# Seven half-size products in part of the first matmul of a fused matmul, GELU, matmul kernel

## The chip, the cores and the metric

The kernel runs on one core of a Trainium2 chip. Times are device microseconds (us) of whole executions. A profiled execution also has a span, from its first to its last recorded instruction, which is some 1.8 us shorter than the time. In these kernels TensorE (PE) does matmuls, VectorE (DVE) and ScalarE (ACT) work elementwise, GpSimd (POOL) mainly issues DMAs, SyncE (SP) issues the rest. A matmul has a stationary operand, which a weight load (PEld in the profile; 577 of them beside 577 matmuls before the change) brings in, and a moving one; its result goes to a bank of PSUM (the `ps` tiles), from where VectorE or ScalarE fetches it. float32r is the 32-bit type that this kernel gives to the operands of products that read sums.

## The reference

```
h = a @ b                    # a 1024x1024, b 1024x2048, float32
h = gelu_tanh(h)
out = h @ c                  # c 2048x1024
```

The tanh form of GELU makes everything between the two products elementwise.

## The kernel before

The intermediate is kept transposed: the first product has b as the stationary operand and the transposed a as the moving one, so its results are tiles of the transposed h, which the second product takes without a transpose. `aT[0]` and `aT[1]` hold the two halves of a's rows, transposed, in bf16. The head loads a's first half and 768 columns of b in float32, casts and transposes, and runs six tiles of the first product k by k as b arrives:

```python
    N0 = 6
    W0 = N0 * 128
    ...
    b0stage = ctx.enter_context(tc.tile_pool(name="b0stage", bufs=8))
    ...
    for k in range(KT):
        if k + 1 < KT:
            cast_b0(k + 1)                      # VectorE casts one half, ScalarE the other
        for t in range(N0):
            nc.tensor.matmul(ps[t], bt(k, t), aT[0][:, k, :],
                             start=(k == 0), stop=(k == KT - 1))
```

The other columns of b, a's second half and c come by casting DMAs on GpSimd's queue. All 256 matmuls of the first product are plain bf16:

```python
    def mm1(t, h):
        p = ppool.tile([128, H], F32, name="ps")
        for k in range(KT):
            nc.tensor.matmul(p, bt(k, t), aT[h][:, k, :],
                             start=(k == 0), stop=(k == KT - 1))
        gelu(t, h, p)
    ...
    for t in range(N0 + N1, NT):                # t = 10 .. 15
        mm1(t, 0)
        if t == NT - 3:
            turn(0)                             # eight transposes on PE, one VectorE copy
        if t == NT - 2:
            turn(1)
            turn(2)
            turn(3)
```

The second product already uses the Winograd form of Strassen's scheme: both operands cut into 2x2 blocks, sums of blocks (`s1` to `s4`, `t1` to `t4`) formed first, and seven block products instead of eight. The sums are float32r tiles; five of the seven products read them, two read bf16 blocks. Its last part is ordered so that one row of output blocks is left, in three narrow pieces, for the end.

Of the kernel before, what the change touches and what calls it, by code (L numbers as in the profile page):

```python
# [9 lines left out]
F32 = mybir.dt.float32  # L10
# [9 lines left out]
def kernel(ctx, tc, a, b, c, out):  # L20
# [9 lines left out]
    W0 = N0 * 128  # L30
    N1 = 4
    W1 = N1 * 128

# [9 lines left out]
    b0stage = ctx.enter_context(tc.tile_pool(name="b0stage", bufs=8))  # L43
# [9 lines left out]
    NH = NT // 2  # L53
    aT = [keep.tile([128, KT, H], BF16, name=f"aT{h}", tag=f"A{h}") for h in range(2)]
    WB = W0 + W1
    b_lo = keep.tile([128, KT, WB], BF16, name="b_lo", tag="B0")
    b_hi = keep.tile([128, KT, N - WB], BF16, name="b_hi", tag="B1")

    def bcols(k0, kn, n0, w):
        if n0 < WB:  # L60
            return b_lo[:, k0:k0 + kn, ds(n0, w)]
        return b_hi[:, k0:k0 + kn, ds(n0 - WB, w)]

    def bt(k, t):
        return bcols(k, 1, t * 128, 128)[:, 0, :]


    hq = [[keep.tile([128, NH, H], F32R if h else BF16, name=f"h{h}{g}") for g in range(2)]
          for h in range(2)]
# [19 lines left out]
    for mt in range(4):  # L89
        load_a0(mt, 2 if mt == 3 else 1)  # L90
# [38 lines left out]
    for mt in range(4):  # L129
        if mt < 3:  # L130
            ab.append(cast_a0(mt + 1))
        turn0(mt, ab[mt], (0,) if mt == 3 else (0, 1))
        if mt < 3:
            warm_up(3)
    cast_b0(0)
    for k in range(KT):
        if k + 1 < KT:
            cast_b0(k + 1)
        for t in range(N0):
            nc.tensor.matmul(ps[t], bt(k, t), aT[0][:, k, :],  # L140
                             start=(k == 0), stop=(k == KT - 1))
# [3 lines left out]
    def gelu(t, h, p):  # L145
        nc.scalar.activation(hq[h][t // NH][:, t % NH, :], p, AF.Gelu_apprx_tanh)  # L146

    for t in range(N0):
        gelu(t, 0, ps[t])


    def load_b(k0, kn, n0, w):
        nc.gpsimd.dma_start(out=bcols(k0, kn, n0, w), in_=bv[:, k0:k0 + kn, ds(n0, w)])

    ps = [(tpool if t < 2 else ppool).tile([128, H], F32, name="pt" if t < 2 else "ps")
          for t in range(N1)]
    for k in range(0, KT, 4):
        load_b(k, 4, W0, W1)
        for i in range(4):
            for t in range(N1):  # L160
                nc.tensor.matmul(ps[t], bt(k + i, N0 + t), aT[0][:, k + i, :],  # L161
                                 start=(k + i == 0), stop=(k + i == KT - 1))
    for t in range(N1):
        gelu(N0 + t, 0, ps[t])


    def mm1(t, h):
        p = ppool.tile([128, H], F32, name="ps")
        for k in range(KT):
            nc.tensor.matmul(p, bt(k, t), aT[h][:, k, :],  # L170
                             start=(k == 0), stop=(k == KT - 1))
        gelu(t, h, p)

    W2 = 384
    for n0 in range(W0 + W1, N, W2):
        for k in range(0, KT, 4):
            load_b(k, 4, n0, W2)

    a1 = []
    for j in range(4):  # L180
        st = abf.tile([128, K], BF16, name="ab1")
        nc.gpsimd.dma_start(out=st, in_=av[:, 4 + j, :])
        a1.append(st)

    def turn(j):
        ab = a1[j]
        pt = tpool.tile([128, KT, 128], BF16, name="pt")
        for k in range(KT):
            nc.tensor.transpose(pt[:, k, :], ab[:, ts(k, 128)], ident)  # L189
        nc.vector.tensor_copy(aT[1][:, :, ts(j, 128)], pt)  # L190

    for t in range(N0 + N1, NT):
        mm1(t, 0)
        if t == NT - 3:
            turn(0)
        if t == NT - 2:
            turn(1)
            turn(2)
            turn(3)
# [7 lines left out]
    (h11, h12), (h21, h22) = hq  # L207
    c11 = keep.tile([128, NH, H], BF16, name="c11")
    c21 = keep.tile([128, NH, H], BF16, name="c21")
    c22 = keep.tile([128, NH, H], F32R, name="c22")  # L210
    c12 = keep.tile([128, NH, H], BF16, name="c12", tag="A0")
# [5 lines left out]
    load_c(c11, 0, 0)  # L217
    load_c(c22, 1, 1)
    load_c(c21, 1, 0)
    load_c(c12, 0, 1)  # L220
# [152 lines left out]
```

## Time and profile before

| | before |
|---|---|
| median time, first three runs | 123.97 us |
| span of the profiled execution | 122.1 us |
| PE busy | 95% of the span |
| first stage (six tiles, k by k) ends | 21.85 us |
| first product ends, second begins | 69.02 us |
| last matmul ends | 119.2 us |

The prediction below shows the page and the chain. The list of waits, cut to PE's own, stands behind the prediction: engine, line, what it waited for, total, times, longest.

```profile
PE ps L101 <- DVE warm L49: 1.2, 1, 1.2
PE ps L140 <- DVE b_lo L125: 0.8, 1, 0.8
PE pt L115 <- DVE aT L118: 0.7, 1, 0.7
PE pt L189 <- DVE aT L190: 0.3, 1, 0.3
```

The first three lie in the head, before 12 us. After it PE really idles once, for 0.3 us, before the transposes of line 189.

The table by half microseconds of the head: the last column is what the DMA engines moved, in GB/s.

```profile
4.50:5.00 0.50, 0.50 (x5) 0.49 (x5) 0.00 (x0) 0.12 (x1) 0.00 (x0) 1.00 0.96 303
...
6.50:7.00 0.50, 0.50 (x10) 0.40 (x8) 0.00 (x0) 0.00 (x0) 0.00 (x0) 1.00 0.83 279
...
9.50:10.00 0.50, 0.41 (x5) 0.21 (x3) 0.05 (x1) 0.50 (x2) 0.00 (x0) 1.00 0.89 237
...
12.50:13.00 0.50, 0.50 (x5) 0.21 (x3) 0.05 (x1) 0.50 (x2) 0.00 (x0) 1.00 1.05 424
```

From 4.5 to 10.5 us the loads run at 237 to 388 GB/s, 312 on average; from 11 to 15.5 us they hold 399 to 424.

### The profile page before, as it was taken

How to read it: one execution, taken by the hardware profiler on the slowest of the kernel's cores; microseconds unless marked ns; L12 is line 12 of the kernel's file. 1: busy time of each engine (PE TensorE's matmuls, PEld its weight loads, DVE VectorE, ACT ScalarE, POOL GpSimd, SP SyncE). 2: the span in 40 equal slices, each digit the busy share in tenths (PEclk: the TensorE clock that was granted, in tenths of full speed). 3: DMA queues.
4: the chain of work that ended last, by engine and by line, in shares of the span. 5: the costliest groups of instructions: out<-in, count | busy, mean ns of one | idle time of the engine just before them, and what ended most of it. 6: DMA issues, size and time to landing. Idle time of an engine off the chain costs nothing.

```text
span 122.1 us, 1486 instructions
## 1 busy us (share of the span) xinstructions
PE 116.1 (95%) x577; PEld 68.3 (56%) x577; DVE 64.6 (53%) x95; ACT 30.7 (25%) x54; POOL 21.5 (18%) x26
## 2 busy tenths in 40 slices
PE   6977999999998999999999999999999999999990
PEld 2542444444456444444444444468888888888880
DVE  0352340000014200006999999999769999974351
ACT  4454752806331133233323331100000000000000
POOL 2000099132440220000000000797000000000000
PEclk9999999999999999999999999999999999999999
DMA  3999969999999999995000000000600022445425
GB/s 144 351 328 347 413 188 191 198 200 205 209 207 206 329 394 231 206 206 97 0 0 0 5 0 3 3 0 0 258 0 0 5 86 86 157 167 191 163 99 167
DMA packets 12582, 18.44 MB, mean 151 GB/s; under 512 B 800, under 2 KB 7584, under 8 KB 12576
## 3 DMA queue, kind: packets, MB, share of 16 engines
q0 software_dynamic: 7968, 8.91, 39.6%
q1 hardware_dynamic: 4464, 9.37, 20.9%
q10 hardware_dynamic: 144, 0.07, 0.2%
q8 instruction: 4, 0.07, 0.2%
q14 instruction: 2, 0.02, 0.0%
HBM read 20.97 MB, written 4.19 MB: 206 GB/s over the span
## 4 chain that ended last, share of the span: by engine, by line
PE 88%; DMA 6%; SPq 2%; DVE 1%; ACT 0%; issue 0%
PE ps L273 41%; PE ps L170 31%; PE ps L140 8%; DMA b_st<-in_b_dram 6%; PE ps L161 3%; PE pt L161 3%; SPq L78 2%; PE pt L189 1%; DVE aT L190 1%; ACT b_lo L126 0%; SPq L85 0%; DVE ot L342 0%; PE pt L115 0%
## 5 line engine op out<-in xcount | busy, mean ns | idle before, releaser
L146 ACT ACTIVATE h<-ps 128x512 fp32r<-128x512 f32 (+1 forms) x30 | 17.3, 602 | 28.6 <-PE ps L170 26.3
L170 PE MATMUL ps<-aT,b_hi 128*128 128x512 bf16 x96 | 21.4, 379 | 0.0
L170 PE MATMUL ps<-aT,b_lo 128*128 128x512 bf16 x80 | 17.4, 379 | 0.0
L170 PEld LDWEIGHTS <-b_hi 128*128 128x128 bf16 x96 | 9.3, 98 | 10.8
L273 PE MATMUL ps<-t,s 128*128 128x512 f32 x64 | 15.0, 392 | 0.0
L273 PE MATMUL ps<-t,h 128*128 128x512 f32 x64 | 14.8, 389 | 0.0
L273 PE MATMUL ps<-c,h 128*128 128x512 bf16 (+2 forms) x80 | 14.2, 336 | 0.0
L313 POOL COPY lk<-u 128x512 f32<-128x512 f32 x1 | 7.7, 7684 | 33.6 <-ACT u L306 33.6
L273 PEld LDWEIGHTS ps<-t,s 128*128 128x128 f32 x64 | 12.0, 188 | 2.6
L273 PEld LDWEIGHTS ps<-t,h 128*128 128x128 f32 x64 | 12.0, 188 | 2.5
L170 PEld LDWEIGHTS <-b_lo 128*128 128x128 bf16 x80 | 7.8, 98 | 9.4
L227 DVE TENSOR_TENSOR t<-c,c 128x1024 fp32r<-128x1024 bf16 x4 | 4.7, 1222 | 15.8 <-DMA c<-in_c_dram 15.7
L190 DVE COPY aT<-pt 128x1024 bf16<-128x1024 bf16 x4 | 2.7, 689 | 19.4 <-PE pt L189 19.3
L140 PE MATMUL ps<-aT,b_lo 128*128 128x512 bf16 x48 | 10.9, 380 | 0.8 <-DVE b_lo L125 0.8
L273 PEld LDWEIGHTS <-h 128*128 128x128 bf16 x80 | 7.2, 98 | 7.0 <-issue 0.3
L140 PEld LDWEIGHTS <-b_lo 128*128 128x128 bf16 x48 | 4.5, 98 | 6.6 <-DVE b_lo L125 1.1
L215 POOL DMA_DIRECT2D c<-in_c_dram x8 | 5.9, 744 | 11.7 <-PE ps L170 6.0
L296 DVE TENSOR_TENSOR ot<-ps,u 128x512 f32<-128x512 f32 x11 | 7.3, 684 | 1.1 <-PE ps L273 1.1
L101 PE MATMUL ps<-warm 128*128 128x512 bf16 x17 | 6.3, 516 | 1.2 <-DVE warm L49 1.2
L273 PE MATMUL ps<-c,s 128*128 128x512 f32 x32 | 7.4, 389 | 0.0
L273 PEld LDWEIGHTS ps<-c,s 128*128 128x128 f32 x32 | 6.0, 188 | 1.2
L125 DVE CAST b_lo<-b_st 128x384 bf16<-128x384 f32 x8 | 2.9, 368 | 5.1 <-DMA b_st<-in_b_dram 5.1
(40 smaller groups left out, 96.5 us busy)
## 6 DMA issues: line engine op xcount, KB each, us to landing
out_dram<-ot SPq DMA_DIRECT2D x15, 256.0 KB, 2.0
c<-in_c_dram POOLq DMA_DIRECT2D x6, 512.0 KB, 14.8
b_st<-in_b_dram SPq DMA_DIRECT2D x7, 384.0 KB, 8.1
c<-in_c_dram POOLq DMA_DIRECT2D x2, 1024.0 KB, 15.0
a_st<-in_a_dram SPq DMA_DIRECT2D x3, 512.0 KB, 4.1
b_hi<-in_b_dram POOLq DMA_DIRECT2D x4, 384.0 KB, 11.3
b_lo<-in_b_dram POOLq DMA_DIRECT2D x2, 512.0 KB, 7.2
ab<-in_a_dram POOLq DMA_DIRECT2D x4, 256.0 KB, 13.9
```

What stands on the lines that cost most here:

```text
L101: nc.tensor.matmul(ps[N0 - 1], warm[:, 0:128], warm, start=True, stop=True)
L125: nc.vector.tensor_copy(b_lo[:, k, 0:HW], b_st[k][:, 0:HW])
L140: nc.tensor.matmul(ps[t], bt(k, t), aT[0][:, k, :], start=(k == 0), stop=(k == KT - 1))
L146: nc.scalar.activation(hq[h][t // NH][:, t % NH, :], p, AF.Gelu_apprx_tanh)
L161: nc.tensor.matmul(ps[t], bt(k + i, N0 + t), aT[0][:, k + i, :], start=(k + i == 0), stop=(k + i == KT - 1))
L170: nc.tensor.matmul(p, bt(k, t), aT[h][:, k, :], start=(k == 0), stop=(k == KT - 1))
L190: nc.vector.tensor_copy(aT[1][:, :, ts(j, 128)], pt)
L215: nc.gpsimd.dma_start(out=dst[:, t:t + 4, :], in_=cv[:, r * NH + t:r * NH + t + 4, ts(q, H)])
L227: nc.vector.tensor_tensor(t1[i], c12[:, ts(i, 2), :], c11[:, ts(i, 2), :], op=SUB)
L273: nc.tensor.matmul(p, lhs(t)[:, ts(j, 128)], rhs(t)[:, q], start=(t == 0), stop=(t == NH - 1))
L296: nc.vector.tensor_tensor(ot, u if swap else p, p if swap else u, op=op)
L313: nc.gpsimd.tensor_copy(last_keep, last)
```

## The change

The intent is fewer matmuls. The left half of the first product (1024 columns of b) stays plain, and all of it is now loaded in the head. The right half (1024 columns) is done as seven block products of 512x512x512, 16 matmuls each, 112 in place of 128. With A and B cut into blocks, `as1` = A21+A22, `as2` = A11-as1, `as3` = A11-A21, `b12` becomes T1 = B12-B11, `bt2` = T1-B22, `bt3` = B22-B12. Two sums get their second addend later, by a DMA that accumulates: `as2` += A12 and `bt2` += B21. The products are combined with VectorE adds from PSUM. In the second product the seven products stay, in another order; the sums t2 and t3 move from VectorE to ScalarE (a negated copy) plus an accumulating DMA, and t4 becomes a further accumulating DMA into t2.

The diff, cut to its core:

```diff
-    W0 = N0 * 128
+    W0 = N // 2                                # columns of b loaded in the head
-    b0stage = ctx.enter_context(tc.tile_pool(name="b0stage", bufs=8))
+    b0stage = ctx.enter_context(tc.tile_pool(name="b0stage", bufs=6))
     ...                                        # (cut: tiles)
+    for j in R:                                # a's second half, first on GpSimd's queue
+        nc.gpsimd.dma_start(out=st, in_=av[:, 4 + j, :])
+    nc.gpsimd.dma_start(out=b12, in_=bv[:, 0:KH, W0 + H:N])
+    nc.gpsimd.dma_start(out=b22, in_=bv[:, KH:KT, W0 + H:N])
     ...                                        # (cut: bx)
+    mm1(6, 0, h11[:, 6, :])
+    turn(0)
+    mm1(7, 0, h11[:, 7, :])
+    turn(1)
+    turn(2)
+    mm1_half(0, 0)                             # 256 columns: needs turn(0), turn(1) only
+    turn(3)
+    mm1_half(1, 0)
+    mm1_half(2, 0)
+    for t in range(3):
+        mm1_half(t, 1)
     ...                                        # (cut: twelve sums on VectorE, mm1 for t = 3 .. 7)
+    for j in R:                                # third product
+        p = bank()
+        prod(p, KH, pairs(bt2), pairs(as2), j)
+        tt(v2[:, j, :], p, v2[:, j, :], op=ADD)
+    for i in range(2):
+        nc.gpsimd.dma_start(out=as2[i], in_=aT[0][:, P2[i + 2], :], accum_op=ADD)
+    for i in range(2):
+        nc.gpsimd.dma_start(out=bt2[i], in_=bx[:, P2[i + 2], :], accum_op=ADD)
+    for j in R:                                # fourth
+        p = bank()
+        prod(p, KH, pairs(bt3), pairs(as3), j)
+        tt(v3[j], p, v2[:, j, :], op=ADD)
     ...                                        # (cut: sums for the second product)
+    for j in R:                                # fifth
+        p = bank()
+        prod(p, KH, whole(b12), pairs(as1), j)
+        add_gelu(h22[:, 4 + j, :], p, v3[j])
+        tt(v2[:, j, :], p, v2[:, j, :], op=ADD)
     ...
+    for j in R:                                # sixth: reads as2 again, with its second addend
+        p = bank()
+        prod(p, KH, whole(b22), pairs(as2), j)
+        add_gelu(h12[:, 4 + j, :], p, v2[:, j, :])
     ...                                        # (cut: seventh, bt2 x a22; the second product)
```

More of the change, by code (lines that the diff above doesn't have):

```diff
@@ L29 @@
     N0 = 6
-    W0 = N0 * 128
-    N1 = 4
-    W1 = N1 * 128
+    W0 = N // 2
+    KH = KT // 2
+    NH = NT // 2
+    R = range(4)
     av = a.rearrange("(mt p) k -> p mt k", p=128)
@@ L51 @@
     make_identity(nc, ident)
-    NH = NT // 2
     aT = [keep.tile([128, KT, H], BF16, name=f"aT{h}", tag=f"A{h}") for h in range(2)]
-    WB = W0 + W1
-    b_lo = keep.tile([128, KT, WB], BF16, name="b_lo", tag="B0")
-    b_hi = keep.tile([128, KT, N - WB], BF16, name="b_hi", tag="B1")
-    def bcols(k0, kn, n0, w):
-        if n0 < WB:
-            return b_lo[:, k0:k0 + kn, ds(n0, w)]
-        return b_hi[:, k0:k0 + kn, ds(n0 - WB, w)]
-    def bt(k, t):
-        return bcols(k, 1, t * 128, 128)[:, 0, :]
-    hq = [[keep.tile([128, NH, H], F32R if h else BF16, name=f"h{h}{g}") for g in range(2)]
-          for h in range(2)]
+    a22 = keep.tile([128, KH, H], F32R, name="a22", tag="A22")
+    b_lo = keep.tile([128, KT, W0], BF16, name="b_lo", tag="B0")
+    bx = keep.tile([128, KT, H], BF16, name="bx", tag="BX")
+    b12 = keep.tile([128, KH, H], F32R, name="b12", tag="BT")
+    b22 = keep.tile([128, KH, H], F32R, name="b22", tag="BR")
+    (h11, h12), (h21, h22) = [[keep.tile([128, NH, H], F32R if h else BF16, name=f"h{h}{g}")
+                               for g in range(2)] for h in range(2)]
     a_st, b_st = {}, {}
@@ L88 @@
     gate = consts.tile([128, 1], F32, name="gate")
-    for mt in range(4):
+    for mt in R:
         load_a0(mt, 2 if mt == 3 else 1)
@@ L128 @@
     ab = [cast_a0(0)]
-    for mt in range(4):
+    for mt in R:
         if mt < 3:
@@ L139 @@
         for t in range(N0):
-            nc.tensor.matmul(ps[t], bt(k, t), aT[0][:, k, :],
+            nc.tensor.matmul(ps[t], b_lo[:, k, ts(t, 128)], aT[0][:, k, :],
                              start=(k == 0), stop=(k == KT - 1))
@@ L143, with gelu, bank @@
             turn0(3, ab[3], (1,))
-    def gelu(t, h, p):
-        nc.scalar.activation(hq[h][t // NH][:, t % NH, :], p, AF.Gelu_apprx_tanh)
+    def gelu(dst, src):
+        nc.scalar.activation(dst, src, AF.Gelu_apprx_tanh)
+    def bank(w=H):
+        return ppool.tile([128, w], F32, name="ps", padded_shape=[128, H])
     for t in range(N0):
-        gelu(t, 0, ps[t])
-    def load_b(k0, kn, n0, w):
-        nc.gpsimd.dma_start(out=bcols(k0, kn, n0, w), in_=bv[:, k0:k0 + kn, ds(n0, w)])
-    ps = [(tpool if t < 2 else ppool).tile([128, H], F32, name="pt" if t < 2 else "ps")
-          for t in range(N1)]
-    for k in range(0, KT, 4):
-        load_b(k, 4, W0, W1)
-        for i in range(4):
-            for t in range(N1):
-                nc.tensor.matmul(ps[t], bt(k + i, N0 + t), aT[0][:, k + i, :],
-                                 start=(k + i == 0), stop=(k + i == KT - 1))
-    for t in range(N1):
-        gelu(N0 + t, 0, ps[t])
-    def mm1(t, h):
-        p = ppool.tile([128, H], F32, name="ps")
-        for k in range(KT):
-            nc.tensor.matmul(p, bt(k, t), aT[h][:, k, :],
-                             start=(k == 0), stop=(k == KT - 1))
-        gelu(t, h, p)
-    W2 = 384
-    for n0 in range(W0 + W1, N, W2):
-        for k in range(0, KT, 4):
-            load_b(k, 4, n0, W2)
+        gelu(h11[:, t, :], ps[t])
     a1 = []
-    for j in range(4):
+    for j in R:
         st = abf.tile([128, K], BF16, name="ab1")
@@ L183 @@
         a1.append(st)
+    nc.gpsimd.dma_start(out=b12, in_=bv[:, 0:KH, W0 + H:N])
+    nc.gpsimd.dma_start(out=b22, in_=bv[:, KH:KT, W0 + H:N])
+    for k in range(0, KT, KH):
+        nc.gpsimd.dma_start(out=bx[:, k:k + KH, :], in_=bv[:, k:k + KH, W0:W0 + H])
     def turn(j):
-        ab = a1[j]
         pt = tpool.tile([128, KT, 128], BF16, name="pt")
         for k in range(KT):
-            nc.tensor.transpose(pt[:, k, :], ab[:, ts(k, 128)], ident)
+            nc.tensor.transpose(pt[:, k, :], a1[j][:, ts(k, 128)], ident)
@@ L190, in turn, with mm1_half @@
         nc.vector.tensor_copy(aT[1][:, :, ts(j, 128)], pt)
-    for t in range(N0 + N1, NT):
-        mm1(t, 0)
-        if t == NT - 3:
-            turn(0)
-        if t == NT - 2:
-            turn(1)
-            turn(2)
-            turn(3)
-    (h11, h12), (h21, h22) = hq
-    c11 = keep.tile([128, NH, H], BF16, name="c11")
-    c21 = keep.tile([128, NH, H], BF16, name="c21")
+        nc.scalar.activation(a22[:, :, ts(j, 128)], aT[1][:, KH:KT, ts(j, 128)], AF.Copy)
+    def mm1_half(t, q):
+        p = bank(256)
+        for k in range(KT):
+            nc.tensor.matmul(p, b_lo[:, k, ts(t, 128)], aT[1][:, k, ts(q, 256)],
+                             start=(k == 0), stop=(k == KT - 1))
+        gelu(h21[:, t, ts(q, 256)], p)
@@ new lines, in mm1, with two @@
+    def mm1(t, h, dst):
+        p = bank()
+        for k in range(KT):
+            nc.tensor.matmul(p, b_lo[:, k, ts(t, 128)], aT[h][:, k, :],
+                             start=(k == 0), stop=(k == KT - 1))
+        gelu(dst, p)
+    mm1(6, 0, h11[:, 6, :])
[9 more added lines that the diff above has]
+        mm1_half(t, 1)
+    tt = nc.vector.tensor_tensor
+    def two(pool, name, tag):
+        return [pool.tile([128, 2, H], F32R, name=name, tag=tag) for _ in range(2)]
@@ new lines @@
+    as3 = two(astage, "as3", "a_st")
+    as1 = two(astage, "as1", "a_st")
+    bt3 = two(b0stage, "bt3", "b0_st")
+    as2 = two(b0stage, "as2", "b0_st")
+    bt2 = two(b0stage, "bt2", "b0_st")
+    P2 = [slice(2 * i, 2 * i + 2) for i in range(4)]
+    for i in range(2):
+        tt(as1[i], aT[1][:, P2[i], :], aT[1][:, P2[i + 2], :], op=ADD)
+    for i in range(2):
+        tt(as2[i], aT[0][:, P2[i], :], as1[i], op=SUB)
+    for i in range(2):
+        tt(as3[i], aT[0][:, P2[i], :], aT[1][:, P2[i], :], op=SUB)
@@ new lines, with whole, pairs, prod @@
+    for i in range(2):
+        tt(bt3[i], b22[:, P2[i], :], b12[:, P2[i], :], op=SUB)
+    for i in range(2):
+        tt(b12[:, P2[i], :], b12[:, P2[i], :], bx[:, P2[i], :], op=SUB)
+    for i in range(2):
+        tt(bt2[i], b12[:, P2[i], :], b22[:, P2[i], :], op=SUB)
+    for t in range(3, NH):
+        mm1(t, 1, h21[:, t, :])
+    def whole(x, t0=0):
+        return lambda t: x[:, t0 + t, :]
+    def pairs(x):
+        return lambda t: x[t // 2][:, t % 2, :]
+    def prod(p, n, lhs, rhs, j, q=slice(0, H)):
+        for t in range(n):
+            nc.tensor.matmul(p, lhs(t)[:, ts(j, 128)], rhs(t)[:, q],
+                             start=(t == 0), stop=(t == n - 1))
@@ L210, with new_out, add_gelu @@
+    def new_out():
+        return opool.tile([128, H], F32, name="ot")
+    def add_gelu(dst, p, u):
+        ot = new_out()
+        tt(ot, p, u, op=ADD)
+        gelu(dst, ot)
+    c11 = keep.tile([128, NH, H], BF16, name="c11", tag="c11")
+    c12 = keep.tile([128, NH, H], BF16, name="c12")
     c22 = keep.tile([128, NH, H], F32R, name="c22")
-    c12 = keep.tile([128, NH, H], BF16, name="c12", tag="A0")
     def load_c(dst, r, q):
@@ L217 @@
     load_c(c11, 0, 0)
+    load_c(c12, 0, 1)
     load_c(c22, 1, 1)
-    load_c(c21, 1, 0)
-    load_c(c12, 0, 1)
-    t1 = [astage.tile([128, 2, H], F32R, name="t1", tag="a_st") for _ in range(4)]
-    t2 = [b0stage.tile([128, 1, H], F32R, name="t2", tag="b0_st") for _ in range(8)]
-    s1 = keep.tile([128, NH, H], F32R, name="s1")
-    def sum_t1(i):
-        nc.vector.tensor_tensor(t1[i], c12[:, ts(i, 2), :], c11[:, ts(i, 2), :], op=SUB)
-    def sum_t2(t):
-        nc.vector.tensor_tensor(t2[t], c22[:, t:t + 1, :], t1[t // 2][:, t % 2:t % 2 + 1, :], op=SUB)
@@ L232, in sum_s1 @@
-    def sum_s1(t):
-        nc.vector.tensor_tensor(s1[:, t, :], h21[:, t, :], h22[:, t, :], op=ADD)
-    for t in range(NT):
-        mm1(t, 1)
-        if 3 <= t < 7:
-            sum_t1(t - 3)
-        if 6 <= t < 10:
-            sum_t2(2 * (t - 6))
-            sum_t2(2 * (t - 6) + 1)
-        if t == WB // 128:
-            t3 = keep.tile([128, NH, H], F32R, name="t3", tag="B0")
-        if t >= NH + 1:
-            sum_s1(t - NH - 1)
-        if WB // 128 <= t < WB // 128 + 4:
-            i = t - WB // 128
-            nc.vector.tensor_tensor(t3[:, ts(i, 2), :], c22[:, ts(i, 2), :], c12[:, ts(i, 2), :], op=SUB)
@@ L249 @@
-    sum_s1(NH - 1)
-    s2 = [keep.tile([128, NH // 2, H], F32R, name=f"s2{g}", tag=f"A{g}") for g in range(2)]
-    def pair(x, i):
-        return x[i // 2][:, ts(i % 2, 2), :]
-    for i in range(4):
-        nc.vector.tensor_tensor(pair(s2, i), s1[:, ts(i, 2), :], h11[:, ts(i, 2), :], op=SUB)
-    for i in range(4):
-        nc.vector.tensor_tensor(h21[:, ts(i, 2), :], h11[:, ts(i, 2), :], h21[:, ts(i, 2), :], op=SUB)
-    s3 = h21
-    def sum_s4(i):
-        nc.vector.tensor_tensor(pair(s2, i), h12[:, ts(i, 2), :], pair(s2, i), op=SUB)
@@ L265, in sum_t4 @@
-    def sum_t4(t):
-        nc.vector.tensor_tensor(t2[t], t2[t], c21[:, t:t + 1, :], op=SUB)
-    def bank(w=H):
-        return ppool.tile([128, w], F32, name="ps", padded_shape=[128, H])
-    def prod(p, lhs, rhs, j, q=slice(0, H)):
-        for t in range(NH):
-            nc.tensor.matmul(p, lhs(t)[:, ts(j, 128)], rhs(t)[:, q],
-                             start=(t == 0), stop=(t == NH - 1))
-    def whole(x):
-        return lambda t: x[:, t, :]
+    v2 = keep.tile([128, 4, H], F32, name="v2", tag="A1")
@@ new lines @@
+    v3 = [abf.tile([128, H], F32, name="v3", tag="ab1") for _ in R]
+    t1 = keep.tile([128, NH, H], F32R, name="t1", tag="B0")
+    def sum_t1(i):
+        tt(t1[:, P2[i], :], c12[:, P2[i], :], c11[:, P2[i], :], op=SUB)
+    for j in R:
+        p = bank()
+        prod(p, KH, whole(bx), whole(aT[0]), j)
+        nc.scalar.activation(v2[:, j, :], p, AF.Copy)
+    for j in R:
+        p = bank()
+        prod(p, KH, whole(bx, KH), whole(aT[0], KH), j)
+        add_gelu(h12[:, j, :], p, v2[:, j, :])
+        if j >= 2:
+            sum_t1(j - 2)
@@ new lines @@
+    for j in R:
+        p = bank()
+        prod(p, KH, pairs(bt2), pairs(as2), j)
+        tt(v2[:, j, :], p, v2[:, j, :], op=ADD)
+        if j >= 2:
+            sum_t1(j)
+    for i in range(2):
+        nc.gpsimd.dma_start(out=as2[i], in_=aT[0][:, P2[i + 2], :], accum_op=ADD)
+    for i in range(2):
+        nc.gpsimd.dma_start(out=bt2[i], in_=bx[:, P2[i + 2], :], accum_op=ADD)
+    for j in R:
+        p = bank()
+        prod(p, KH, pairs(bt3), pairs(as3), j)
+        tt(v3[j], p, v2[:, j, :], op=ADD)
@@ new lines, with sum_t2 @@
+    t2 = [astage.tile([128, 2, H], F32R, name="t2", tag="a_st") for _ in R]
+    def sum_t2(i):
+        nc.scalar.mul(t2[i], c22[:, P2[i], :], -1.0)
+        nc.gpsimd.dma_start(out=t2[i], in_=t1[:, P2[i], :], accum_op=ADD)
+    for i in (0, 1):
+        sum_t2(i)
+    for j in R:
+        p = bank()
+        prod(p, KH, whole(b12), pairs(as1), j)
+        add_gelu(h22[:, 4 + j, :], p, v3[j])
+        tt(v2[:, j, :], p, v2[:, j, :], op=ADD)
+    for i in (2, 3):
+        sum_t2(i)
+    for j in R:
+        p = bank()
+        prod(p, KH, whole(b22), pairs(as2), j)
+        add_gelu(h12[:, 4 + j, :], p, v2[:, j, :])
@@ new lines, with sum_s1, t3p, t3t @@
+    s1 = {}
+    def sum_s1(i):
+        s1[i] = b0stage.tile([128, 2, H], F32R, name="s1", tag="b0_st")
+        tt(s1[i], h21[:, P2[i], :], h22[:, P2[i], :], op=ADD)
+    sum_s1(2)
+    sum_s1(3)
+    t3b = keep.tile([128, KH, H], F32R, name="t3b", tag="BT")
+    def t3p(i):
+        return t3[i] if i < 2 else t3b[:, P2[i - 2], :]
+    def t3t(t):
+        return t3[t // 2][:, t % 2, :] if t < 4 else t3b[:, t - 4, :]
+    def sum_t3(i):
+        nc.scalar.mul(t3p(i), c12[:, P2[i], :], -1.0)
+        nc.gpsimd.dma_start(out=t3p(i), in_=c22[:, P2[i], :], accum_op=ADD)
@@ L279, in halves @@
+    sum_t3(2)
+    sum_t3(3)
+    for j in R:
+        p = bank()
+        prod(p, KH, pairs(bt2), whole(a22), j)
+        add_gelu(h22[:, j, :], p, v3[j])
+    sum_s1(0)
+    sum_s1(1)
+    s2 = [keep.tile([128, KH, H], F32R, name=f"s2{g}", tag=tag) for g, tag in ((0, "A0"), (1, "BR"))]
+    for i in (2, 3, 0, 1):
+        tt(s2[i // 2][:, P2[i % 2], :], h11[:, P2[i], :], s1[i], op=SUB)
     def halves(x):
         return lambda t: x[t // 4][:, t % 4, :]
-    def pairs(x):
-        return lambda t: x[t // 2][:, t % 2, :]
@@ L285, in ones, with combine @@
-    def ones(x):
-        return lambda t: x[t][:, 0, :]
-    def new_out():
-        return opool.tile([128, H], F32, name="ot")
     def store(ot, m, q0, w=H, queue=nc.sync):
         queue.dma_start(out=out[ts(m, 128), ds(q0, w)], in_=ot[:, 0:w])
-    def combine(m, q, p, u, op=ADD, swap=False):
+    def combine(m, q, p, u):
         ot = new_out()
-        nc.vector.tensor_tensor(ot, u if swap else p, p if swap else u, op=op)
+        tt(ot, p, u, op=ADD)
         store(ot, m, q * H)
-    R = range(4)
@@ L300 @@
-    u2 = [abf.tile([128, H], F32, name="u2", tag="ab1") for _ in R]
-    u3 = keep.tile([128, 4, H], F32, name="u3", tag="B1")
+    p1 = keep.tile([128, 4, H], F32, name="p1", tag="A22")
+    p5 = keep.tile([128, 4, H], F32, name="p5", tag="A1")
+    u2 = keep.tile([128, 4, H], F32, name="u2", tag="c11")
+    u3 = [abf.tile([128, H], F32, name="u3", tag="ab1") for _ in R]
+    t3 = two(b0stage, "t3", "b0_st")
+    for i in (0, 1):
+        sum_t3(i)
     for j in R:
         p = bank()
-        prod(p, whole(h11), whole(c11), j)
-        nc.scalar.activation(u2[j], p, AF.Copy)
+        prod(p, NH, whole(h11), whole(c11), j)
+        nc.scalar.activation(p1[:, j, :], p, AF.Copy)
@@ new lines @@
+    c21 = keep.tile([128, NH, H], BF16, name="c21", tag="BX")
+    load_c(c21, 1, 0)
+    for j in R:
+        p = bank()
+        prod(p, NH, pairs(s1), whole(t1), j)
+        nc.scalar.activation(p5[:, j, :], p, AF.Copy)
+    for i in R:
+        tt(h21[:, P2[i], :], h11[:, P2[i], :], h21[:, P2[i], :], op=SUB)
+    s3 = h21
+    for j in R:
+        p = bank()
+        prod(p, NH, halves(s2), pairs(t2), j)
+        tt(u2[:, j, :], p, p1[:, j, :], op=ADD)
+        tt(p5[:, j, :], u2[:, j, :], p5[:, j, :], op=ADD)
@@ L307 @@
+    for i in R:
+        sp = s2[i // 2][:, P2[i % 2], :]
+        tt(sp, sp, h12[:, P2[i], :], op=ADD)
+    for i in R:
+        nc.gpsimd.dma_start(out=t2[i], in_=c21[:, P2[i], :], accum_op=ADD)
+    for j in R:
+        p = bank()
+        prod(p, NH, whole(s3), t3t, j)
+        tt(u3[j], p, u2[:, j, :], op=ADD)
+        combine(4 + j, 1, p, p5[:, j, :])
     for j in range(3):
         p = bank()
-        prod(p, whole(h12), whole(c21), j)
-        combine(j, 0, p, u2[j])
-    last = u2[3]
@@ L312 @@
-    last_keep = opool.tile([128, H], F32, name="lk", bufs=1)
-    nc.gpsimd.tensor_copy(last_keep, last)
+        prod(p, NH, whole(h12), whole(c21), j)
+        combine(j, 0, p, p1[:, j, :])
     for j in R:
         p = bank()
-        prod(p, halves(s2), ones(t2), j)
-        nc.vector.tensor_tensor(u2[j], p, u2[j], op=ADD)
+        prod(p, NH, halves(s2), whole(c22), j)
+        combine(j, 1, p, p5[:, j, :])
     for j in R:
         p = bank()
-        prod(p, whole(s3), whole(t3), j)
-        nc.vector.tensor_tensor(u3[:, j, :], p, u2[j], op=ADD)
-        sum_s4(j)
@@ L323 @@
-    for j in R:
-        p = bank()
-        prod(p, whole(s1), pairs(t1), j)
-        combine(4 + j, 1, p, u3[:, j, :])
-        nc.vector.tensor_tensor(u2[j], p, u2[j], op=ADD)
-        sum_t4(2 * j)
-        sum_t4(2 * j + 1)
-    for j in R:
-        p = bank()
-        prod(p, halves(s2), whole(c22), j)
-        combine(j, 1, p, u2[j])
-    for j in R:
-        p = bank()
-        prod(p, whole(h22), ones(t2), j)
-        combine(4 + j, 0, p, u3[:, j, :], op=SUB, swap=True)
+        prod(p, NH, whole(h22), pairs(t2), j)
@@ L338 @@
+        combine(4 + j, 0, p, u3[j])
     for q0, w, queue in ((0, 256, nc.sync), (256, 128, nc.scalar), (384, 128, nc.sync)):
         p = bank(w)
-        prod(p, whole(h12), whole(c21), 3, q=ds(q0, w))
+        prod(p, NH, whole(h12), whole(c21), 3, q=ds(q0, w))
         ot = new_out()
-        nc.vector.tensor_tensor(ot[:, 0:w], p, last_keep[:, ds(q0, w)], op=ADD)
+        tt(ot[:, 0:w], p, p1[:, 3, ds(q0, w)], op=ADD)
         store(ot, 3, q0, w, queue)
```

## The prediction

The sum came to -2.1 us (-2.6 + 0.6 - 0.4 + 0.3); of the accumulating DMAs, their zero is the author's estimate. Some is estimate: that the weight load is what widens float32r's spacing (98 and 188 ns, 215.8 and 226.6 ns are in the trace, the link was not tested); that casting loads read about 400 GB/s, twice the 195 to 207 that the windows from 22 to 30 us show; that VectorE lags by up to 3.5 us, which six banks cover, from its 24 us against PE's 21.

> **What bounds the kernel now.** I read the page first for each engine's share, then the chain that ended last in order of time, then the groups of instructions by shape for durations, then half-microsecond windows for the transfers. The page:
>
> ```profile
> span 122.1 us, 1486 instructions
> PE 116.1 (95%) x577; PEld 68.3 (56%) x577; DVE 64.6 (53%) x95; ACT 30.7 (25%) x54; POOL 21.5 (18%) x26
> ...
> PE   6977999999998999999999999999999999999990
> DVE  0352340000014200006999999999769999974351
> PEclk9999999999999999999999999999999999999999
> DMA  3999969999999999995000000000600022445425
> ```
>
> TensorE (PE) is full from the fifth slice to the last but one, at full granted clock. VectorE (DVE) is near full only in the second half; the DMA engines are full in the first half and nearly idle after it. A busy PE need not be a fast one, so I looked at the chain, whose columns are start, duration and what ran:
>
> ```profile
> 3.58 7.39 DMA b_st<-in_b_dram
> ...
> 12.62 9.23 PE ps L140 x42
> ...
> 28.75 6.91 PE ps L170 x32
> ...
> 38.32 0.70 DVE aT L190
> ...
> 39.67 29.35 PE ps L170 x136
> 69.02 50.17 PE ps L273 x240
> 119.20 0.02 issue
> 119.22 0.29 DVE ot L342
> ```
>
> Up to 12.62 the input loads lead. From there to 119.2 the chain is matmuls, with one break: about 0.7 us at 38.3, where a transpose waits for VectorE. So the time is PE's instruction count times its spacing, plus the head (12.6) and the tail (2.9). The spacings come from the chain: 29.35/136 = 0.2158 us for a bf16 matmul of 512 columns. For float32r I take the windowed timeline of the second product: its 64 matmuls between 88.23 and 102.73 take 14.50 us, 0.2266 us each, 5% more. The groups by shape point to why: the weight load.
>
> ```profile
> L170 PE MATMUL ps<-aT,b_lo 128*128 128x512 bf16 x80 | 17.4, 379 | 0.0
> L170 PEld LDWEIGHTS <-b_lo 128*128 128x128 bf16 x80 | 7.8, 98 | 9.4
> L273 PEld LDWEIGHTS ps<-t,h 128*128 128x128 f32 x64 | 12.0, 188 | 2.5
> L263 DVE TENSOR_TENSOR s<-h,s 128x1024 fp32r<-128x1024 bf16 x4 | 4.9, 1216 | 0.0
> L296 DVE TENSOR_TENSOR ot<-ps,u 128x512 f32<-128x512 f32 x11 | 7.3, 684 | 1.1 <-PE ps L273 1.1
> ```
>
> The 379 is a pipelined latency, not a spacing. Pairs of VectorE operations overlap a little: eight of 128x512 ran in 4.90 us (0.61 each) and four of 128x1024 in 4.62 (1.15 each).
>
> [...] Loads behind a queue took 7 to 15 us to landing here, and no trace yet has an accumulating DMA.
>
> **The change part by part.**
>
> *Matmuls.* The second product already uses seven half-size products and keeps 160 float32r, 56 bf16 and 24 narrow matmuls, only in another order. New is the first product's right half (1024 columns of b): 8 x 16 = 128 bf16 matmuls become 7 x 16 = 112. Two of the seven stay bf16 (32 matmuls), five are float32r (80). Before: 128 x 0.2158 = 27.6 us. After: 32 x 0.2158 + 80 x 0.2266 = 6.9 + 18.1 = 25.0. **PE gains 2.6 us, not the 3.5 that 16 saved bf16 matmuls would give**; 0.86 goes back to the slower weights. [...]
>
> *Head.* The first stage now loads 1024 columns of b for each k, not 768: 512 KB in place of 384. In the windows from 11 to 15.5 us DMA moves about 410 GB/s; b tiles are cast at 12.19, 13.16, ... 18.01, 0.97 apart, so the new spacing is 1.29 us. PE needs 6 x 0.2158 = 1.295 for a k, so loads now just keep up instead of running ahead. k=1 comes 0.65 us later (12.84), its casts take about 0.47 on VectorE and 0.63 on ScalarE (scaled from 368 and 523 ns), and the stage ends about 22.4 to 22.6 instead of 21.85. **Cost 0.6 us.** Six staging buffers for eight are harmless: the seventh load waits for the cast of the first at about 12 us, well ahead of its turn at 19.
>
> *The first a block transposed.* The second half of a comes first on the GpSimd queue. It reads 2.1 MB; the source side of a casting load moves about 400 GB/s (200 of bf16 written), so 5.2 us from about 18.5, landed by 26 to 27. PE asks for its four parts at about 24.2, 26.4, 26.9 and 28.5: met. The wait for VectorE's copy falls from 0.7 to about 0.3 us. **Gain 0.4 us, counted with low confidence.** b12, b22 and bx (4.2 MB) follow by about 37 us; their matmuls start at about 42.
>
> *VectorE.* Twelve sums of 128x1024 for the first product, 12 x 1.15 = 14 us, run from about 30 to 44 while PE does plain matmuls; bt2 is needed at 49. Then from 46.6 to 70.6 come 24 PSUM adds (14.6 us) and six sums (6.9), and four more sums: about 24 us of VectorE work against 21 us of PE work. It lags PE by up to 3.5 us, which six PSUM banks just cover. **Cost 0 to 0.5 us.**
>
> *Accumulating DMAs.* as2 and bt2 get their second addend by DMA. as2 may be touched once the third product is done (about 52.5) and is needed two products later, 32 x 0.2266 = 7.3 us. [...] The others (t2, t3, t4) have over 10 us. **Cost 0 expected, the largest risk.** The 7.7 us GpSimd copy that goes away was off the chain.
>
> Sum: -2.6 + 0.6 - 0.4 + 0.3 = -2.1 us. The median of before is 123.97, so **121.9; I put 122.1** for small unseen waits.
>
> **The rivals.**
>
> 1. *An accumulate too slow.* If two land only after 9 or 10 us, PE stands 2 to 3 us ahead of the product that reads as2, and the time is 124 to 125. For it: nothing here has measured such a DMA, [...] and c's loads share its queue until about 52. Against: [...] a nearly empty DMA after 52.
> 2. *VectorE becomes the bound between 46 and 74 us.* Its 24 us against 21 say it could; a longer lag means waits for PSUM banks, 123 to 124. Against: the following 7 us of plain products need almost no VectorE.
> 3. *Loads late in the head.* GpSimd's queue starts at the landing of the fifth b tile, some 3.7 us before the last b tile lands (2.9 before). If both queues share evenly, the first stage ends 1 us later and the time is about 123.
> 4. *All hidden.* Without any new wait and with the old break gone, 121.3: the most that I can find, just over 2%.
>
> **Range and chances.** The arithmetic of PE is firm to 0.3 us. The waits are one-sided: up to 0.6 better, up to 3 worse. So 120.7 to 124.3. 2% faster means below 121.5, which needs every wait hidden: 0.25. Slower by 2% means above 126.5, which needs two rivals at once: 0.07. The rest is within 2%.
>
> **What would show it.** In the changed profile: 80 more float32r matmuls and 96 fewer bf16 ones in units of 512 columns, at 0.2266 and 0.2158; the first stage's end near 22.5; no PE idle over 0.3 us before the product that reads as2; idle of PE named after VectorE or PSUM small; the last product ending about 2 us earlier than 119.2. Wrong would be a chain that goes through a DMA into as2 or bt2, or through VectorE adds between 46 and 74 us, or a head several microseconds later. A gain beyond 3 us would mean that float32r matmuls run at bf16 spacing here, or that some wait of before which I take for PE work has gone.

## The result, and the profile after

| | before | after |
|---|---|---|
| median time, six runs each | 123.99 us | 122.66 us |
| ratio, 95% interval | | 0.9897 [0.9866, 0.9928] |
| span of the profiled execution | 122.1 | 120.8 |
| first stage ends | 21.85 | 22.93 |
| last matmul ends | 119.2 | 117.85 |

A ratio is the mean time of one kernel's runs over that of the other's runs of the same rounds, so not quite the ratio of the medians. The change is 1.0% faster: within 2%, and inside the predicted range; 122.1 was the predicted time.

The page of the changed kernel, to be read against that of before:

```profile
PE 113.2 (94%) x579; PEld 75.9 (63%) x585; DVE 81.8 (68%) x111; ACT 46.3 (38%) x77; POOL 26.5 (22%) x39
...
PE   6967799998999999999999999999999999999990
...
DVE  0343223026999963999999999995789992824350
...
DMA  4899999999999999909999999999996999954424
```

PE is as full as before and works less. VectorE is now nearly full from a quarter of the span on, and the DMA engines work almost to the end, because sums have become DMAs. The chain that ended last, in order of time:

```profile
13.69 9.24 PE ps L132 x42
22.93 0.43 PE ps L174 x2
...
24.66 0.45 PE pt L160 x8
...
27.32 0.70 DVE aT L161
...
29.56 4.37 PE ps L167 x40
...
96.61 21.24 PE ps L233 x110
```

It is PE from 13.69 to 117.85, with the same kind of break at a transpose's copy as before. The list of waits, cut to those of PE for the casts of b and at the break:

```profile
PE ps L132 <- DVE b_lo L117: 1.3, 2, 0.9
PE ps L132 <- ACT b_lo L118: 0.4, 1, 0.4
PE ps L167 <- DVE aT L161: 0.3, 1, 0.3
```

In the head PE waits 1.7 us for b's casts, against 0.8 before; at the break it is 0.3 us, as before. The order of PE's own instructions gives the length of the new part: start, length to the last result, group.

```profile
42.40 7.07 PE L233 MATMUL ps<-aT,bx 128*128 128x512 bf16 x31
49.12 7.63 PE L233 MATMUL ps<-as,bt 128*128 128x512 f32 x32
56.58 7.42 PE L233 MATMUL ps<-as,b 128*128 128x512 f32 x32
63.84 3.79 PE L233 MATMUL ps<-a,bt 128*128 128x512 f32 x16
67.47 7.08 PE L233 MATMUL ps<-c,h 128*128 128x512 bf16 x31
```

The seven block products take 67.47 - 42.40 = 25.07 us, start to start, and no group starts late. (One of the first 32 matmuls is missing from the records.) Before the change 128 bf16 matmuls at 0.2158 us stood there, 27.6 us.

Where the time went, then: 2.55 us saved in the block products, 1.08 lost in the head in this pair of profiles. The break and its transposes cost the same: before, 39.67 - 35.66 less eight matmuls (1.73) is 2.28 us; after, 29.56 - 24.66 less eight matmuls and eight half-width ones (1.73 + 0.87; 40 of these take 4.37 us in the chain, 0.109 each) is 2.30. The net of -1.4 is what the last matmul's end shows (-1.35).

### The profile page after: what moved, and what is told of

It reads as the page before. It is cut to its first block, busy times and chain, and to the rows that moved or that the text cites. A ratio compares the mean times of both kernels' runs of the same rounds, so it can differ in the third digit from the quotient of the medians. Undisturbed runs are those within 1.5% of the kernel's fastest.

```text
span 120.8 us, 1587 instructions
## 1 busy us (share of the span) xinstructions
PE 113.2 (94%) x579; PEld 75.9 (63%) x585; DVE 81.8 (68%) x111; ACT 46.3 (38%) x77; POOL 26.5 (22%) x39
## 2 busy tenths in 40 slices
DMA packets 13831, 28.41 MB, mean 235 GB/s; under 512 B 1024, under 2 KB 5504, under 8 KB 13824
## 3 DMA queue, kind: packets, MB, share of 16 engines
q1 hardware_dynamic: 4464, 10.42, 23.3%
## 4 chain that ended last, share of the span: by engine, by line
PE 85%; DMA 7%; SPq 3%; DVE 1%; issue 1%
PE ps L233 62%; PE ps L174 10%; PE ps L132 8%; DMA b_st<-in_b_dram 7%; PE ps L167 4%; SPq L70 2%; PE pt L160 1%; SPq L77 1%; DVE aT L161 1%; DVE b_lo L117 0%; DVE ot L404 0%
## 5 line engine op out<-in xcount | busy, mean ns | idle before, releaser
L241 DVE TENSOR_TENSOR ot<-ps,v 128x512 f32<-128x512 f32 x16 | 10.4, 683 | 3.2 <-PE ps L233 3.2
L174 PE MATMUL ps<-aT,b_lo 128*128 128x512 bf16 x54 | 12.5, 379 | 0.1
L138 ACT ACTIVATE h<-ps 128x512 bf16<-128x512 f32 (+2 forms) x19 | 9.4, 536 | 8.3 <-PE ps L174 6.2
L132 PE MATMUL ps<-aT,b_lo 128*128 128x512 bf16 x47 | 10.7, 379 | 1.6 <-DVE b_lo L117 1.3
L138 ACT ACTIVATE h<-ot 128x512 bf16<-128x512 f32 (+1 forms) x16 | 9.4, 622 | 5.9 <-DVE ot L241 5.9
L349 DVE TENSOR_TENSOR ot<-ps,p 128x512 f32<-128x512 f32 x11 | 7.5, 688 | 4.8 <-PE ps L233 2.7
L117 DVE CAST b_lo<-b_st 128x512 bf16<-128x512 f32 x8 | 3.4, 426 | 7.0 <-DMA b_st<-in_b_dram 7.0
L233 PE MATMUL ps<-as,bt 128*128 128x512 f32 x32 | 7.6, 396 | 0.0
L233 PE MATMUL ps<-as,b 128*128 128x512 f32 x32 | 7.4, 389 | 0.0
L118 ACT ACTIVATE b_lo<-b_st 128x512 bf16<-128x512 f32 x8 | 5.0, 630 | 5.5 <-DMA b_st<-in_b_dram 5.3
L233 PE MATMUL ps<-aT,bx 128*128 128x512 bf16 x31 | 7.0, 379 | 0.1
```

What stands on the lines that cost most here:

```text
L117: nc.vector.tensor_copy(b_lo[:, k, 0:HW], b_st[k][:, 0:HW])
L118: nc.scalar.activation(b_lo[:, k, HW:W0], b_st[k][:, HW:W0], AF.Copy)
L132: nc.tensor.matmul(ps[t], b_lo[:, k, ts(t, 128)], aT[0][:, k, :], start=(k == 0), stop=(k == KT - 1))
L138: nc.scalar.activation(dst, src, AF.Gelu_apprx_tanh)
L174: nc.tensor.matmul(p, b_lo[:, k, ts(t, 128)], aT[h][:, k, :], start=(k == 0), stop=(k == KT - 1))
L233: nc.tensor.matmul(p, lhs(t)[:, ts(j, 128)], rhs(t)[:, q], start=(t == 0), stop=(t == n - 1))
```

## The experiments

The theory: the gain is the count of matmuls times their spacing, all of it on PE's chain; the head takes part of it back because its loads grew; VectorE and the accumulating DMAs are hidden, but only just. The rivals: VectorE or the accumulating DMAs eat some of the gain; the head's loss is chance. Twelve runs were made, four on each of three chips: eight altered kernels, three of these a second time, and the changed kernel again; all their results matched the reference. The record shows no run of the changed kernel on the chip of the first four, so what these say of it rests mainly on their traces.

**The right half done plainly again** (`e_plain`).

```diff
-    (seven block products, their sums, the two accumulations)
+    def right(dst, bb, h, j):
+        p = bank()
+        prod(p, KT, whole(bb), whole(aT[h]), j)
+        gelu(dst, p)
+    # bx and by (the last 512 columns, bf16) against aT[0], then aT[1]
```

> The changed kernel with the right half of the first product done plainly again (128 bf16 matmuls in place of 32 bf16 and 80 float32r; no sums, no accumulating DMAs for it); head and order otherwise as in the changed kernel. Theory A (the gain is only the count of matmuls times their spacing, 2.6 us): 2.4 to 2.8 us slower than the changed kernel, about 125.2 us, so 1.0 to 1.4 us slower than the kernel before. Rival B (the new sums and accumulating DMAs cost PE waits that eat part of the gain): the difference to the changed kernel is under 2 us. The first stage ends near 22.9 us in both theories if the longer head is systematic, near 22.4 if the last half microsecond of it was chance.

Measured: 125.33 us, ratio to before 1.0105 [1.0076, 1.0134]. PE's order in its trace:

```profile
42.14 7.07 PE L212 MATMUL ps<-aT,bx 128*128 128x512 bf16 x31
49.04 13.98 PE L212 MATMUL ps<-aT,by 128*128 128x512 bf16 x63
62.86 7.07 PE L212 MATMUL ps<-aT,bx 128*128 128x512 bf16 x31
69.76 6.42 PE L212 MATMUL ps<-c,h 128*128 128x512 bf16 x29
```

The same stretch takes 69.76 - 42.14 = 27.62 us, 2.55 more than in the changed kernel. That is theory A, to a twentieth of a microsecond: nothing of the gain is eaten by waits. It also shows that the rest of the change, without the block products, is 1.0% slower than before.

**bf16 temporaries in the first product** (`e_bf16`). Meant to be less exact, by how much was not measured; the check against the reference still passes, by what margin was not recorded.

```diff
-    a22 = keep.tile([128, KH, H], F32R, name="a22", tag="A22")
+    a22 = keep.tile([128, KH, H], BF16, name="a22", tag="A22", padded_shape=[128, KT, H])
     # likewise b12, b22, and as1, as2, as3, bt2, bt3
```

> The sums and the copies of a22, b12, b22 in the first product in bf16 instead of float32r, so that all 112 of its matmuls run in bf16 (less exact; the comparison with the reference may fail on purpose). Theory A (the float32r spacing takes back 0.86 us of the 3.5 that 16 saved matmuls give): 0.8 to 0.95 us faster than the changed kernel, about 121.8 us. Rival (PE is held by VectorE or by the accumulating DMAs in that stretch, so that the spacing does not count): under 0.3 us.

Measured: 121.60 us, ratio 0.9804 [0.9774, 0.9834]. PE's order in its trace:

```profile
42.01 7.07 PE L233 MATMUL ps<-aT,bx 128*128 128x512 bf16 x31
62.73 3.58 PE L233 MATMUL ps<-a,bt 128*128 128x512 bf16 x15
66.36 7.07 PE L233 MATMUL ps<-c,h 128*128 128x512 bf16 x32
```

The stretch takes 66.36 - 42.01 = 24.35 us, 0.72 less than the changed kernel, where 0.86 was worked out and 0.8 to 0.95 expected. So float32r's wider spacing is a real cost on the chain; about a sixth less of it came back than the count says. The shortfall lies in the seventh product: it takes 66.36 - 62.73 = 3.63 us, no less than with float32r (67.47 - 63.84), because of one pause of some 0.2 us in it, for which the profile names no cause.

**The narrow head** (`e_head768`): 768 columns of b in the head as before the change, the other 256 by one casting DMA.

```diff
-        st = b0stage.tile([128, W0], F32, name="b0_st")
-        w = W0 // parts
+        st = b0stage.tile([128, WS], F32, name="b0_st", padded_shape=[128, W0])   # WS = 768
+        w = WS // parts
     ...
+    nc.gpsimd.dma_start(out=b_lo[:, :, WS:W0], in_=bv[:, :, WS:W0])               # ahead of a1
```

> Only 768 columns of b are loaded and cast in the head, as before the change; the other 256 come as one casting DMA, first on GpSimd's queue. Theory H (the wider loads set the head, 1.08 us in the profiles): the first stage ends near 21.85 us again and the time falls by 0.5 to 1.1 us, unless a's second half then comes late. Rival (the head's delay is chance of a run or due to the six buffers): the stage still ends near 22.9 and nothing is gained.

Measured: 121.47 us, ratio 0.9809 [0.9772, 0.9846]. In the chain the last 42 matmuls of the first stage are

```profile
12.31 9.24 PE ps L133 x42
```

so the stage ends at 21.55 us, and from there to the last matmul the kernel takes 94.93 us, as the changed one does (117.85 - 22.93 = 94.92). So the wide head costs what it delays the first stage by, and nothing after it absorbs the delay. Six buffers are kept here, so they are not the cause.

**The second addends on VectorE** (`e_dve`).

```diff
-        nc.gpsimd.dma_start(out=as2[i], in_=aT[0][:, P2[i + 2], :], accum_op=ADD)
+        tt(as2[i], as2[i], aT[0][:, P2[i + 2], :], op=ADD)
     # likewise bt2 += bx
```

> The second addends of as2 and bt2 added by VectorE (four sums of 128x1024, 4.6 us) instead of by accumulating DMAs. Theory V (VectorE lags PE in that stretch and PSUM banks only just cover it): 2 to 4 us slower than the changed kernel, with PE waiting for VectorE between 58 and 75 us. Rival (VectorE has room there; the DMA is not needed): within 0.5 us of the changed kernel.

Measured: 127.99 us, ratio 1.0337 [1.0313, 1.0362]: some 5.3 us over the changed kernel, more than the 4.6 us of work added. PE's order, and then the clock by windows (the third column from the right is the granted clock):

```profile
56.31 1.98 PE L233 MATMUL ps<-as,b 128*128 128x512 f32 x8
61.84 7.32 PE L233 MATMUL ps<-as,b 128*128 128x512 f32 x24 [3.55 <-DVE v L287]
68.99 3.79 PE L233 MATMUL ps<-a,bt 128*128 128x512 f32 x16
```

```profile
62.00:63.00 1.00, 1.00 (x4) 0.76 (x5) 1.00 (x3) 0.00 (x0) 0.00 (x0) 0.60 1.03 197
63.00:64.00 1.00, 1.00 (x4) 0.81 (x3) 1.00 (x2) 0.00 (x0) 0.00 (x0) 0.50 1.02 197
64.00:65.00 1.00, 1.00 (x4) 0.81 (x3) 1.00 (x3) 0.63 (x1) 0.00 (x0) 0.50 0.02 0
65.00:66.00 1.00, 1.00 (x4) 0.76 (x4) 1.00 (x3) 0.60 (x1) 0.00 (x0) 0.69 0.00 0
```

PE waits 3.55 us for VectorE's adds of the fourth product (line 287), which empty the PSUM banks that it needs; then its clock is halved for some microseconds, which costs 0.40 + 0.50 + 0.50 + 0.31 = 1.7 us more. From start to start the wait costs 3.7 us (61.84 - 56.31, less eight matmuls), and 3.7 + 1.7 is the 5.4 us by which this span (126.2) exceeds that of the changed kernel. Theory V is right about the cause, and my size for it left out the clock. The clock fell some 0.4 us after PE had begun again (estimated from the mean of 0.60 in the window from 62 us). All five executions of this kernel had a mean granted clock of 0.986 or 0.987, all six of the changed kernel 0.997 or 1.0; that the idle time is what brings the clock down is read from this and from the order in time, and was not tested alone.

**The changed kernel once more** (`e_again`), on the next chip.

> The changed kernel once more, unaltered, as the base of this chip and for a second profile of its head. Theory H (wide loads set the head): the first stage ends between 22.5 and 22.9 us, 0.7 to 1.1 later than before the change. Rival (0.6 us as predicted, the rest of the 1.08 of the first profile chance): about 22.4. Time 122.3 to 122.8 us.

Measured: 121.98 us, ratio 0.9853 [0.9824, 0.9883], against 0.9897 in its first runs: the intervals overlap. The time is below the 122.3 to 122.8 that was expected. So effects of half a per cent are judged below from traces and from runs on one chip. The first stage ends at 22.59, and the rest takes 117.53 - 22.59 = 94.94 us, as in the first profile to 0.02. What varies in the traces is the head.

**The accumulated operand wanted one product sooner** (`e_swap`).

```diff
-    (fifth product: b12 x as1)
-    (sixth product: b22 x as2)
+    (b22 x as2, added into v2)
+    (b12 x as1: h22 from v3, h12 from v2)
```

> The product that reads as2 a second time is moved one product (3.6 us) earlier, ahead of the one that it followed; same instructions otherwise. In the trace of the changed kernel the two accumulating DMAs into as2 land 4.1 and 5.7 us after issue, at about 57.1 and 59.3 us, and the moved product would want the second at about 57.0. Theory D (the accumulate is hidden only by the two products placed between): PE waits about 2.3 us on a DMA, 2.0 to 2.6 us slower than the changed kernel. Rival (the landing has slack for a whole product): within 0.5 us.

Measured: 126.16 us, ratio 1.0174 [1.0134, 1.0215]; its span is 4.0 us over that of the changed kernel on the same chip.

```profile
48.73 7.65 PE L233 MATMUL ps<-as,bt 128*128 128x512 f32 x32
56.84 0.70 PE L233 MATMUL ps<-as,b 128*128 128x512 f32 x2 [0.46 <-DMA as<-aT]
58.96 8.73 PE L233 MATMUL ps<-as,b 128*128 128x512 f32 x30 [1.42 <-DMA as<-aT]
```

PE waits 0.46 and 1.42 us for the two DMAs into as2. From start to start they cost more, 0.62 (56.84 - 48.73 is 8.11 us, against 7.49 in the changed kernel on this chip) and 1.67 (58.96 - 56.84, less two matmuls), together the 2.3 that was expected. The rest, which was not expected, is the clock again: it is at 0.78, 0.50, 0.50 and 0.52 of full speed in the four microseconds from 59, a loss of 1.7 us. The clock does not fall each time: one of the four executions kept its mean granted clock at 1.0, against 0.985 or 0.986 in the others, and took 125.19 us, about 1 us less than they. So theory D holds: the two products in between are what hides the accumulations. In the changed kernel these take 4.1 and 5.7 us from issue to landing, and those into bt2, issued behind them at 54.2 and 54.8 us, take 7.2 and 8.7 and land at about 61.4 and 63.5. bt2 is the stationary operand of the seventh product, whose weight loads begin at 63.61; the third of them, at about 64.1, reads the second part of bt2: 0.6 us is left. as2 is a moving operand; its second part is read by the third matmul of the sixth product, at about 60.6, against 59.3: 1.3 us is left.

**No half-width tiles** (`e_nohalf`).

```diff
     turn(2)
-    mm1_half(0, 0)
     turn(3)
-    mm1_half(1, 0)
     ...
-    for t in range(3, NH):
+    for t in range(NH):
         mm1(t, 1, h21[:, t, :])
```

> The six half-width tiles are undone: all four transposes of a's second half first, then eight tiles of full width. Theory (the halves cover VectorE's copies of the third and fourth transpose): PE idles for about 0.35 us before the fourth transpose and 0.7 to 0.8 us before the first tile, 0.6 to 1.0 us slower than the changed kernel. Rival (the half-width tiles gain nothing): within 0.3 us.

Measured: 122.87 us, 0.7% over the changed kernel on the same chip (ratios 0.9924 and 0.9853). PE's waits name the place:

```profile
PE ps L174 <- DVE aT L161: 0.8, 1, 0.8
PE pt L160 <- DVE aT L161: 0.3, 1, 0.3
```

Without the halves, the first full tile needs VectorE's copy of the last transpose and waits 0.8 us for it. Before the change that wait did not exist, because a tile of the other half of a came next. The halves pay for themselves, but only by avoiding a wait that the new order would have made.

**The two gains together** (`e_best`, and once more beside its parts as `e_best2`, `e_head768b`, `e_bf16b`): both edits above in one kernel.

> Both alterations that gained: head of 768 columns and bf16 temporaries in the first product. If the two gains lie in different stages of one chain of PE work they add up: 1.1 plus 0.7 to 1.0 us off the changed kernel, 120.6 to 120.9 us, 2.4 to 2.7% under the kernel before. If they overlap: about 121.4.

Measured: 121.16 us, ratio 0.9779 [0.9743, 0.9814], beside 0.9853 for the changed kernel on the same chip. That is 0.8 us by the medians, not the 1.8 hoped for, and the single runs spread from 120.32 to 121.49. The profiled one was the fastest: there the last matmul ends at 115.72, the full 1.8 us before that of the changed kernel on this chip (117.53).

> The combination of narrow head and bf16 temporaries again, now beside its two parts on one chip. If the gains add up: 0.6 to 1.0 us faster than the narrow head alone and 0.9 to 1.2 faster than bf16 alone. If not, it is within 0.3 us of the better part.

> The narrow head alone again, on the chip of the combination; first stage's end near 21.5 us, time 121.0 to 121.6.

> The bf16 temporaries alone again, on the chip of the combination; first product's right half in 24.3 us instead of 25.1, time 121.2 to 121.8.

Measured: 120.78 us (0.9766 [0.9739, 0.9793]) for both, 121.65 (0.9847 [0.9814, 0.9879]) for the narrow head alone, 121.56 (0.9855 [0.9821, 0.9889]) for bf16 alone. The combination is 0.9 us faster than the one and 0.8 than the other (0.9 to 1.2 was expected for the second): the gains are separate, but each is nearer to 0.8 us than to 1.1. The trace of the narrow head on this chip shows why it varies:

```profile
22.80 1.90 PE L176 MATMUL ps<-aT,b_lo 128*128 128x512 bf16 x8 [0.89 <-DMA b_lo<-in_b_dram]
```

PE is through with the first stage at 21.9 us and waits 0.9 us for the 256 columns that were moved to GpSimd's queue; in the first profile of the same kernel this wait is absent. The stage itself ends a little later than the 21.5 expected. The narrow head exchanges a sure delay for one that comes in some executions.

**Everything in bf16** (`e_all`): the combination, with the second product's float32r tiles in bf16 as well (`F32R = mybir.dt.bfloat16`).

> The combination, with every float32r tile of the second product in bf16 too (less exact; the comparison with the reference may fail). If the float32r spacing costs there what it costs in the first product, 160 matmuls x 10.8 ns: 1.5 to 1.8 us faster than the combination.

Measured: 118.79 us, ratio 0.9627 [0.9600, 0.9655], 1.7 us (by the ratios) to 2.0 us (by the medians) under the combination, about what the spacing says, and still accepted by the comparison. This is the fastest version, and what exactness it loses was not measured. It is a trade of precision and not a finding about the change.

## Why the prediction was right or wrong

- **What bounds the kernel**: right. PE's chain explains the time before and after, and in the profiled executions every experiment moved the end by what it added to or took from PE's chain.
- **Matmuls, -2.6 us**: right, -2.55 (25.07 us against 27.62 in the plain version). The split of that term, 3.5 less 0.86 for float32r, is right in kind; bf16 gave back 0.72. (Of the half-width tiles, the trace has 40 in 4.37 us, 0.109 each: 48 take 5.2 us, as do the 24 matmuls of the three tiles that they replace, 24 x 0.2158.)
- **Head, +0.6 us**: mechanism right, size too small. 1.08 in the two first profiles; over all eight profiles with the wide head the stage ends between 22.05 and 22.93, 22.55 on average, over all six with the narrow one (that of before among them) between 21.30 and 21.91, 21.69 on average: 0.86 us. The step that failed is "k=1 comes 0.65 us later (12.84)". It divided the extra 262 KB by 405 GB/s, the rate after 11 us, though most of them are moved before. At the 312 GB/s that the windows of before average from 4.5 to 10.5 us they take 0.84 (an estimate from those rows). That the lower rate is the whole reason was not tested. In the first pair k=1 came 1.07 us later (13.69 against 12.62), and there the loads also moved only 164 and 123 GB/s in the two windows from 4.5 us, against 303 and 295 before; no other profile is that low there, so that pair may be an extreme case. The prediction's third rival named a stage that ends 1 us later, but by another way, the two queues sharing the last loads: the 42 matmuls from k=1 on take 9.24 us, as before (9.23), so nothing came late after k=1.
- **The break, -0.4 us**: wrong; the gain is nil. The step read the chain's piece "DVE aT L190, 0.70" as idle time of PE. Part of that copy ran beside the third transpose, and the idle was 0.3 us, as the list of waits before the change says; after, it is 0.3 us again.
- **VectorE, 0 to 0.5 us**: the lower end. PE does not wait for it in the new stretch. That it has no room to spare was right: 4.6 us more of it cost 5.3. (The 24 us of VectorE work should be 26 by its own terms, 14.6 + 6.9 + 4 x 1.15; in the 24 us from 46.6 to 70.6 the trace has VectorE busy for 23.3.)
- **Accumulating DMAs, 0 expected**: right, but no run before had shown such a DMA, so it was an estimate. They are hidden narrowly: the prediction put the risk on as2, which has 1.3 us to spare, while bt2 behind it has 0.6.
- **The sum**: -2.6 + 0.6 - 0.4 + 0.3 = -2.1 was predicted, -1.33 measured in the medians. In that pair of profiles the head is 0.5 and the break 0.4 worse than their terms and VectorE 0.3 better: 0.6 of the 0.8 between the two. The 0.2 added for unseen waits (122.1 in place of 121.9) went the right way for no reason that the runs show. That the time came within 0.6 us of the forecast is partly luck: this 0.2 and the unused 0.3 for VectorE made up for about half of what the head and the break had wrong.

## What to carry to other kernels

Price a saved matmul by the spacing of the type that replaces it (here 0.2266 us and not 0.2158), and read a wait from the list of waits, since a piece of the chain on another engine may run beside work (here 0.70 us in the chain, 0.3 of it a wait). When an operation moves to a DMA to relieve an engine, count what stands between its issue and its reader: here two products hid it, and with one product fewer the loss was nearly twice the wait in the profiled execution (4.0 us against 2.3), because PE's clock fell too; three of the four executions had the lower clock. A load that grew in the head was paid in full here, so price it by the rate in the windows in which it moves (here 312 GB/s) and not by the best rate of the page (here 405).

## What else the runs measured

- Spacing: float32r matmuls of 512 columns follow each other at 226.6 ns (64 in 14.50 us), against 215.8 for bf16 (136 in 29.35 us), with weight loads of 188 and 98 ns.
- Clock: in the profile of `e_swap` gaps of 0.46 and 1.42 us with two matmuls between them, 2.6 us from the last full product to the next, were followed by four microseconds at 0.78, 0.50, 0.50 and 0.52 of full clock; in that of `e_dve` one gap of 3.55 us was followed by four at 0.60, 0.50, 0.50 and 0.69. Another execution of `e_swap` kept a mean clock of 1.0. What length of gap it takes was not tested.
- Accumulating DMAs between two tiles of the kernel: four of them issued in a row, 0.5 MB of float32r written by each, landed 4.1, 5.7, 7.2 and 8.7 us after their issue, while the DMA engines moved 254 GB/s in the window from 55 to 60 us. With bf16 destinations (`e_bf16`), half as large, the medians were 3.8 us for the two into as2 and 5.6 for the two into bt2, against 4.9 and 7.9.
